# Complex product of the convolutions in three VectorE instructions, and five row buffers for the last experts

## The chip, the cores and the metric

One core of a Trainium2 chip runs the whole kernel. The metric is the device time of one execution in microseconds (us): the median of several runs. A program this long is decided by stages: TensorE (PE) multiplies matrices and reads its weights through a second track (PEld), VectorE (DVE), ScalarE (ACT) and GpSimd (POOL) do elementwise work, SyncE (SP) issues transfers, and GpSimd issues those with indices.

## The reference

Three layers on 1024 tokens of width 1024, all in float32. First an attention layer (MLA), then a layer of long convolutions (Hyena), then a block that mixes sliding window attention with a gated recurrence and ends in a mixture of 32 experts. The change touches two places.

The long convolution, done twice (`spec` comes from filters that a small network produces):

```python
def fft_long_conv(u, spec):
    L = u.shape[1]
    U = jnp.fft.rfft(u.astype(jnp.float32), n=2 * L, axis=1)
    return jnp.fft.irfft(U * spec, n=2 * L, axis=1)[:, :L].astype(u.dtype)
```

The experts: each token goes to two of 32 experts; an expert computes `silu(x @ w_gate) * (x @ w_up)` and multiplies it by `w_down`; the weighted rows are summed per token.

```python
def expert_block(args):
    xb, e = args
    h = jax.nn.silu(xb @ w_gate[e]) * (xb @ w_up[e])
    return h @ w_down[e]
```

## The kernel before

Nearly every matrix product is done as three: each float32 operand is split into a high part (rounded to the type that TensorE takes at full rate) and a low remainder. The helper `hilo` does this with a ScalarE copy (line 165) and a VectorE subtraction (line 166); `mm3` issues the three matmuls (lines 187 to 189).

The order of the instructions on each engine is fixed before the run, by a planner that simulates the program with costs of its own and issues what is ready there. `tc.issue_after(x)` adds an edge that keeps an engine's instructions behind `x` on that engine. Every engine works through its own list in order.

**Convolutions** (function `fwd`, `inv0`, `inv1`). Channels come in four chunks of 256 and two orders, eight units `n`. A forward transform `fwd(n, t)`, half of a unit (16 halves in all), makes four frequency tiles. For each, TensorE writes a PSUM tile `z` of 128 x 2 x 256 (real and imaginary parts) with 24 matmuls of 256 columns; there are four such PSUM tiles. SyncE loads the spectrum tile `K` (three buffers), and VectorE forms the complex product `yf` (lines 1177 to 1185): two half products into `B`, a full product, a subtraction for the real part, an addition for the imaginary part (with a sign for the last two tiles of eight). GpSimd then does six butterfly instructions on the four tiles (lines 1190 to 1196), `hilo` splits the results into `yh` and `yl`, and the inverse transform of the unit (`inv0` into `acc`, or `inv1` into `bcc`) takes them as matmul operands. The loop runs `fwd(n, 0)`, the inverse of unit n - 1, then `fwd(n, 1)`, so `fwd(n, 1)` and `fwd(n + 1, 0)` follow each other. When the convolutions end, TensorE goes on with the output projection (`oz`), whose weights `owr` are loaded and split at that time.

**Experts** (function `expert`, a generator that the loop at line 2069 steps so that experts overlap). For expert `e`, GpSimd gathers up to 112 rows of the normalised activations into `xg` (line 2003, two buffers), TensorE transposes them (line 2011), six weight blocks of 1 MB each are loaded and split, `ez` holds gate and up products, `dz` the two halves of the down product. ScalarE copies `dz`, scaled, from PSUM into the rows `y` (line 2047), and GpSimd adds the rows to the output with an indirect, accumulating transfer (line 2048). These additions go to the same tensor and are kept in order, each after the landing of the one before. PSUM has five banks for `ez` and `dz` together. From about the tenth expert on, `y` lies in one of three buffers of a weight pool (`praw[0]`, which holds no weights by then); before that it lies in a pair of its own (`px`).

In the last experts GpSimd's list holds only gathers and additions. After expert 31 a loop handles experts with more than 112 rows; its count is read at run time.

Of the kernel before, what the change touches and what calls it, by code (L numbers as in the profile page):

```python
# [8 lines left out]
F32 = mybir.dt.float32  # L9
# [3 lines left out]
AF = mybir.ActivationFunctionType  # L13
# [131 lines left out]
def _build(es, tc, nc, a, stop, dbg):  # L145
# [968 lines left out]
    with stc, ExitStack() as st:  # L1114
# [50 lines left out]
        def fwd(n, t):  # L1165

            c, o = units[n]
            y = []
            for ft in (t, 2 + t, 4 + t, 6 + t):
                z = ps.tile([P, 2, 256], F32, tag="z", name="z")  # L1170
                for q in range(2):
                    for kt in range(4):
                        mm3(z[:, q], *fwd_c(q, ft, kt), sd[n][q][0][:, kt], sd[n][q][1][:, kt], kt == 0, kt == 3)
                K = pk.tile([P, 2, 256], F32, tag="K", name="K", bufs=3)
                k_in.append(SY.dma_start(K, spec[c, o, ft].rearrange("p (r h) -> p r h", r=2)).ins)
                B = pk.tile([P, 2, 256], F32, tag="B", name="B")
                V.tensor_tensor(B[:, 0], z[:, 0], K[:, 1], ALU.mult)
                V.tensor_tensor(B[:, 1], z[:, 1], K[:, 0], ALU.mult)
                y.append(pyf.tile([P, 2, 256], F32, tag="yf", name="yf"))
                V.tensor_tensor(y[-1], z, K, ALU.mult)  # L1180
                V.tensor_tensor(y[-1][:, 0], y[-1][:, 0], y[-1][:, 1], ALU.subtract)
                if ft < 6:
                    V.tensor_tensor(y[-1][:, 1], B[:, 0], B[:, 1], ALU.add)
                else:
                    V.scalar_tensor_tensor(y[-1][:, 1], B[:, 0], -1.0, B[:, 1], ALU.mult, ALU.subtract)

            out = []
            E = V if n == 7 and t else G
            d = pyf.tile([P, 2, 256], F32, tag="yd", name="yd", bufs=1)
            E.tensor_tensor(d, y[1], y[3], ALU.add)  # L1190
            E.tensor_tensor(y[1], y[1], y[3], ALU.subtract)
            E.tensor_tensor(y[3], y[0], d, ALU.subtract)
            E.tensor_tensor(y[0], y[0], d, ALU.add)  # L1193
            d = pyf.tile([P, 2, 256], F32, tag="yd", name="yd", bufs=1)
            E.tensor_tensor(d, y[2], y[1], ALU.add)
            E.tensor_tensor(y[2], y[1], y[2], ALU.subtract)
            for x in (y[0], y[3], d, y[2]):
                yh = py.tile([P, 2, 256], F32R, tag="yh", name="yh")
                yl = py.tile([P, 2, 256], F32R, tag="yl", name="yl")
                hilo(yh, yl, x)  # L1200
                out.append((yh, yl))
            ys[n].append(out)
# [780 lines left out]
    def expert(px, pw, praw, ps, pst, xg, ix, wt, e, static=True):  # L1983

        def src(w):

            w = (w[e] if static else w[bass.ds(e, 1)].rearrange("o d f -> (o d) f")).rearrange("(p k) f -> p (k f)", p=P)
            return w[:, :2048], w[:, 2048:]

        def load(w):  # L1990
            n = n_raw[0]
            n_raw[0] += 1
            raw = slot_of(n).tile([P, 4, 512], F32, tag="ewr", name="ewr")
            if n in GATE:
                V.tensor_copy(raw[:, 0, :1], GATE[n])
            SY.dma_start(raw.rearrange("p k f -> p (k f)"), w)
            hi = pw[n % 5].tile([P, 4, 512], F32R, tag="ewh", name="ewh")
            lo = pw[n % 5].tile([P, 4, 512], F32R, tag="ewl", name="ewl")
            m = 1 if n < 5 else 2
            for k in range(0, 4, m):  # L2000
                hilo(hi[:, k:k + m], lo[:, k:k + m], raw[:, k:k + m])
            return hi, lo
        G.indirect_dma_start(out=xg[:BR], out_offset=None, in_=hn_d, in_offset=bass.IndirectOffsetOnAxis(ap=ix[:BR], axis=0),  # L2003
                             bounds_check=1023, oob_is_err=False)
        xh = px.tile([P, 8, P], F32R, tag="xh", name="xh")
        xl = px.tile([P, 8, P], F32R, tag="xl", name="xl")
        xk = xg.rearrange("t (p k) -> t k p", k=8)
        for k4 in range(2):
            z = pst.tile([P, 4, P], F32, tag="tr", name="tr")
            for k in range(4):  # L2010
                T.transpose(z[:, k], xk[:, k4 * 4 + k], ident)  # L2011
            hilo(xh[:, k4 * 4:k4 * 4 + 4], xl[:, k4 * 4:k4 * 4 + 4], z)
        yield
        zz = []
        for w in (wg, wu):
            z = ps.tile([P, 512], F32, tag="mm", name="ez")
            for k4 in range(2):
                wh, wl = load(src(w)[k4])
                for k in range(4):
                    kk = k4 * 4 + k  # L2020
                    mm3(z, xh[:, kk], xl[:, kk], wh[:, k], wl[:, k], kk == 0, kk == 7)
                if w is wg or k4 == 0:
                    yield
            zz.append(z)
        h = px.tile([P, 512], F32, tag="h", name="h", bufs=1)
        S.activation(h, zz[0], AF.Silu)
        V.tensor_tensor(h, h, zz[1], ALU.mult)  # L2027
        yield
        hh = px.tile([P, 4, P], F32R, tag="hh", name="hh", bufs=1)
        hl = px.tile([P, 4, P], F32R, tag="hl", name="hl", bufs=1)  # L2030
        z = pst.tile([P, 4, P], F32, tag="tr", name="tr")
        hk = h.rearrange("t (p k) -> t k p", k=4)
        for k in range(4):
            T.transpose(z[:, k], hk[:, k], ident)
        hilo(hh, hl, z)
        yield
        if n_raw[0] < 62:
            y = px.tile([P, 1024], F32, tag="y", name="y")
        else:
            y = praw[0].tile([P, 4, 512], F32, tag="ewr", name="y")[:, :2].rearrange("p a c -> p (a c)")  # L2040
        zz = [ps.tile([P, 512], F32, tag="mm", name="dz") for _ in range(2)]
        ws = [load(w) for w in src(wd)]
        for c, k in ((0, 0), (1, 0), (0, 1), (1, 1), (0, 2), (0, 3), (1, 2), (1, 3)):
            wh, wl = (x[:, k % 2 * 2 + c] for x in ws[k // 2])
            mm3(zz[c], hh[:, k], hl[:, k], wh, wl, k == 0, k == 3)
            if k == 3:
                S.activation(y[:BR, c * 512:(c + 1) * 512], zz[c][:BR], AF.Copy, scale=wt[:BR])
        G.indirect_dma_start(out=out_d, out_offset=bass.IndirectOffsetOnAxis(ap=ix[:BR], axis=0), in_=y[:BR], in_offset=None,  # L2048
                             bounds_check=1023, oob_is_err=False, compute_op=ALU.add)
        yield  # L2050

    ps = pool("ps8", 5, PSUM, st8)
    pst = pool("ps8t", 3, PSUM, st8)
    n_raw = [0]
    pw = [pool(f"ew{j}", 1, st=st8) for j in range(5)]

    def slot_of(n):
# [66 lines left out]
```

## Time and profile before

| | |
|---|---|
| median of 3 runs | 3218.64 us (3216.76 to 3223.12) |
| profiled execution | 3216.41 us, its span 3214.6 us |
| TensorE busy | 3053.7 us, 95% |
| VectorE busy | 2294.8 us, 71% |
| ScalarE busy | 1607.8 us, 50% |
| GpSimd busy | 892.2 us, 28% |
| mean granted TensorE clock | 0.985 |
| convolutions, from the first to the last `z` | about 1382 to 1664 us |
| experts, from the first gate product to the last addition | 2600.5 to 3202 us |

The shares are means over stages with different limits, so a stage is read by itself. Matmuls are pipelined: a row shows each from its start to its modelled end, and the next starts before that, so TensorE is not at its full rate wherever it is "busy". In the lists, a bracket says how long the engine was idle before an instruction and what ended that.

### The profile page before, as it was taken

The numbers are of one execution on the slowest core, as the hardware profiler recorded it, in microseconds if no ns is written. First come the engines' busy times: TensorE is split into PE (matmuls) and PEld (weight loads), VectorE is DVE, ScalarE is ACT, GpSimd is POOL, SyncE is SP. The second block draws the span as 40 slices with busy tenths as digits, with TensorE's granted clock in tenths as the row PEclk, the third lists the DMA queues.
The fourth block names the chain that finished last, engine by engine and source line by source line (L and its number), as shares of the span: only waits on it lengthen the run. The fifth ranks groups of instructions, "written<-read, shape, count | busy, mean of one in ns | idle before, by whom it ended". The sixth has DMA issues, their size and how long they took to land. (4 is left out here: it accounts for less than half of the span.)

```text
span 3214.6 us, 49325 instructions
## 1 busy us (share of the span) xinstructions
PE 3053.7 (95%) x18106; PEld 2681.9 (83%) x18106; DVE 2294.8 (71%) x4600; ACT 1607.8 (50%) x2762; POOL 892.2 (28%) x825
## 2 busy tenths in 40 slices
PE   7998999999999899999988999999999989999997
PEld 3898879998887788899987999888878978878775
DVE  4575236666667988889896667577646689889885
ACT  3333347666653444411134446455423368778785
POOL 3771042775001444456650000000000025331111
PEclk9999999999999999999999999999999989999998
DMA  8752222331224222174335311321444689999995
GB/s 276 214 193 86 79 92 63 91 99 61 83 92 120 85 101 99 60 255 143 106 108 189 98 52 53 107 66 60 124 148 163 214 302 365 340 345 365 372 363 168
DMA packets 287019, 514.58 MB, mean 160 GB/s; under 512 B 49594, under 2 KB 201826, under 8 KB 262200
## 3 DMA queue, kind: packets, MB, share of 16 engines
q1 hardware_dynamic: 273608, 478.60, 43.8%
q0 software_dynamic: 13168, 32.81, 3.8%
q8 instruction: 143, 2.34, 0.3%
q14 instruction: 100, 0.82, 0.1%
HBM read 431.28 MB, written 92.61 MB: 163 GB/s over the span
## 5 line engine op out<-in xcount | busy, mean ns | idle before, releaser
L166 DVE TENSOR_TENSOR ewl<-ewr,ewh 128x1024 fp32r<-128x1024 f32 (+1 forms) x394 | 447.1, 1192 | 49.2 <-ACT ewh L165 48.3
L165 ACT ACTIVATE ewh<-ewr 128x1024 fp32r<-128x1024 f32 (+1 forms) x394 | 377.8, 1034 | 33.2 <-PE dz L189 24.6
L187 PE MATMUL ez<-ewh,xh 128*128 128x512 f32 x512 | 203.8, 401 | 10.4 <-DVE h L2027 5.2
L188 PE MATMUL ez<-ewl,xh 128*128 128x512 f32 x512 | 203.9, 398 | 3.5 <-DVE ewl L166 3.3
L189 PE MATMUL ez<-ewh,xl 128*128 128x512 f32 x512 | 201.3, 393 | 0.0
L187 PE MATMUL cz<-cTh,w5h 128*128 128x512 f32 x384 | 152.5, 399 | 0.8 <-ACT w5h L165 0.8
L188 PE MATMUL cz<-cTl,w5h 128*128 128x512 f32 x384 | 152.5, 397 | 0.0
L189 PE MATMUL cz<-cTh,w5l 128*128 128x512 f32 x384 | 150.2, 395 | 0.0
L166 DVE TENSOR_TENSOR ptl<-tr,pth 128x512 fp32r<-128x512 f32 x160 | 108.0, 686 | 49.0 <-ACT pth L165 48.4
L2003 POOL DMA_INDIRECT xg<-hn_d,idx x32 | 51.0, 1594 | 313.2 <-PE tr L2011 311.8
L798 DVE TENSOR_SCALAR_CACHE_REDUCE pr<-s 128x512 f32<-128x512 f32 (+1 forms) x192 | 109.6, 597 | 34.5 <-PE s L797 18.6
L187 PEld LDWEIGHTS ez<-ewh,xh 128*128 128x128 f32 x512 | 97.2, 190 | 34.1 <-ACT xh L165 7.6
L768 POOL TENSOR_SCALAR adaw<-adaw,cond 128x256 f32<-128x256 f32 x112 | 103.9, 940 | 54.4 <-DMA adaw<-in_ada_w_dram 54.4
L188 PEld LDWEIGHTS ez<-ewl,xh 128*128 128x128 f32 x512 | 97.4, 190 | 23.8 <-DVE ewl L166 4.9
L165 ACT ACTIVATE pth<-tr 128x512 fp32r<-128x512 f32 x160 | 91.6, 592 | 49.5 <-PE tr L815 47.9
L189 PEld LDWEIGHTS ez<-ewh,xl 128*128 128x128 f32 x512 | 97.0, 190 | 19.9
L187 PE MATMUL oz<-owh,oh 128*128 128x512 f32 x256 | 102.1, 403 | 10.7 <-ACT oh L165 5.1
L165 ACT ACTIVATE yh<-yf 128x512 fp32r<-128x512 f32 x48 | 28.5, 625 | 157.3 <-POOL yf L1193 141.7
L802 ACT ACTIVATE pr<-pr,mx 128x1280 f32<-128x1280 f32 x64 | 87.2, 1362 | 32.7 <-DVE mx L801 32.4
L189 PE MATMUL oz<-owh,ol 128*128 128x512 f32 x256 | 101.0, 399 | 1.5 <-DVE ol L166 1.5
L188 PE MATMUL oz<-owl,oh 128*128 128x512 f32 x256 | 101.9, 400 | 0.5 <-DVE owl L166 0.5
L188 PE MATMUL dz<-ewl,hh 128*128 128x512 f32 x256 | 100.5, 393 | 0.0
(770 smaller groups left out, 10896.0 us busy)
## 6 DMA issues: line engine op xcount, KB each, us to landing
ewr<-in_w_up_experts_dram SPq DMA_DIRECT2D x64, 1024.0 KB
ewr<-in_w_gate_experts_dram SPq DMA_DIRECT2D x64, 1024.0 KB
ewr<-in_w_down_experts_dram SPq DMA_DIRECT2D x64, 1024.0 KB
spec<-so SPq DMA_DIRECT2D x64, 256.0 KB
adaw<-in_ada_w_dram SPq DMA_DIRECT2D x64, 256.0 KB
hwr<-in_hy_w_in_dram SPq DMA_DIRECT2D x64, 256.0 KB
K<-spec SPq DMA_DIRECT2D x64, 256.0 KB
w5r<-in_w_in_dram SPq DMA_DIRECT2D x60, 256.0 KB
```

What stands on the lines that cost most here:

```text
L165: S.activation(hi, x, AF.Copy)
L166: V.tensor_tensor(lo, x, rd(hi), ALU.subtract)
L187: T.matmul(ps, lh, rh, start=first, stop=False)
L188: T.matmul(ps, lh, rl, start=False, stop=False)
L189: return T.matmul(ps, ll, rh, start=False, stop=last)
L768: G.tensor_scalar(w[:, i], w[:, i], cond[:, k + i, 0:1], None, ALU.mult)
L798: V.tensor_scalar(pr[:, k0:k0 + n], z[:, :n], 1.0, None, ALU.mult, ALU.max, accum_out=mx[:, c:c + 1])
L802: S.activation(pr, pr, AF.Exp, scale=SC, bias=mx[:, 3:4], accum_out=sm)
L2003: G.indirect_dma_start(out=xg[:BR], out_offset=None, in_=hn_d, in_offset=bass.IndirectOffsetOnAxis(ap=ix[:BR], axis=0), bounds_check=1023, ...
```

## The change

Convolutions: the spectrum tile gets a third column block of 256, which takes a negated copy of the imaginary part (for the last two tiles of eight, the negated real part, and the imaginary part is negated in place). ScalarE makes these copies. VectorE then forms the product in three instructions over 512 elements each: real part of `z` times the pair, imaginary part times the turned pair (written back into `z`, in PSUM), and the sum. The buffer `B` is gone.

Experts: the additions are collected in a list `done`. From the gather that is issued when 28 additions are listed on (experts 30 and 31), a gather is kept behind the sixth addition from the end of the list, which is that of expert 22 or 23. Of the experts from 24 on, 26, 28 and 31 take their rows `y` from the pair `px`, the others from the three buffers of `praw[0]`.

```diff
-                K = pk.tile([P, 2, 256], F32, tag="K", name="K", bufs=3)
-                k_in.append(SY.dma_start(K, spec[c, o, ft].rearrange("p (r h) -> p r h", r=2)).ins)
-                B = pk.tile([P, 2, 256], F32, tag="B", name="B")
-                V.tensor_tensor(B[:, 0], z[:, 0], K[:, 1], ALU.mult)
-                V.tensor_tensor(B[:, 1], z[:, 1], K[:, 0], ALU.mult)
+                K = pk.tile([P, 3, 256], F32, tag="K", name="K", bufs=3)
+                u = 1 if ft < 6 else 0
+                k_in.append(SY.dma_start(K[:, u:u + 2], spec[c, o, ft].rearrange("p (r h) -> p r h", r=2)).ins)
+                if u:
+                    S.activation(K[:, 0], K[:, 2], AF.Copy, scale=-1.0)
+                else:
+                    S.activation(K[:, 2], K[:, 0], AF.Copy, scale=-1.0)
+                    S.activation(K[:, 1], K[:, 1], AF.Copy, scale=-1.0)
                 y.append(pyf.tile([P, 2, 256], F32, tag="yf", name="yf"))
-                V.tensor_tensor(y[-1], z, K, ALU.mult)
-                V.tensor_tensor(y[-1][:, 0], y[-1][:, 0], y[-1][:, 1], ALU.subtract)
-                if ft < 6:
-                    V.tensor_tensor(y[-1][:, 1], B[:, 0], B[:, 1], ALU.add)
-                else:
-                    V.scalar_tensor_tensor(y[-1][:, 1], B[:, 0], -1.0, B[:, 1], ALU.mult, ALU.subtract)
+                V.tensor_tensor(y[-1], z[:, 0:1].broadcast_to([P, 2, 256]), K[:, u:u + 2], ALU.mult)
+                V.tensor_tensor(z, z[:, 1:2].broadcast_to([P, 2, 256]), K[:, 1 - u:3 - u], ALU.mult)
+                V.tensor_tensor(y[-1], z, y[-1], ALU.add)
...
-        G.indirect_dma_start(out=xg[:BR], out_offset=None, in_=hn_d, in_offset=bass.IndirectOffsetOnAxis(ap=ix[:BR], axis=0),
-                             bounds_check=1023, oob_is_err=False)
+        with tc.issue_after(done[-6].ins) if static and len(done) > 27 else ExitStack():
+            G.indirect_dma_start(out=xg[:BR], out_offset=None, in_=hn_d, in_offset=bass.IndirectOffsetOnAxis(ap=ix[:BR], axis=0),
+                                 bounds_check=1023, oob_is_err=False)
...
-        if n_raw[0] < 62:
+        if n_raw[0] < 62 or (static and e > 23 and e % 5 in (1, 3)):
             y = px.tile([P, 1024], F32, tag="y", name="y")
...
-        G.indirect_dma_start(out=out_d, ...
+        done.append(G.indirect_dma_start(out=out_d, ...
```

## Rows read from the trace of the kernel before

**Rows 1.** Stretch: busy us (instructions) of PE, PEld, DVE, ACT, POOL; clock, DMA.
```profile
1400.00:1672.00 272.00, 255.40 (x2072) 251.92 (x2070) 244.69 (x412) 50.75 (x83) 167.97 (x132) 0.99 0.38 123
```

**Rows 2.** TensorE's waits, 1400 to 1672: us in total, times, longest.
```profile
PE bcc L189 <- DVE yl L166: 6.2, 5, 1.9
PE z L187 <- DVE yf L1180: 4.3, 3, 1.7
PE acc L188 <- DVE yl L166: 3.3, 4, 1.8
PE bcc L187 <- ACT yh L165: 1.9, 1, 1.9
```

**Rows 3.** VectorE's groups, 1380 to 1690: busy us, mean ns; last, line 1180's durations.
```profile
L1180 DVE TENSOR_TENSOR yf<-z,K 128x512 f32<-128x512 f32 x64 | 43.5, 679 | 0.0
L1183 DVE TENSOR_TENSOR yf<-B 128x256 f32<-128x256 f32 x48 | 42.1, 876 | 1.1
...
L1181 DVE TENSOR_TENSOR yf<-yf 128x256 f32<-128x256 f32 x64 | 39.0, 609 | 1.2
L1177 DVE TENSOR_TENSOR B<-z,K 128x256 f32<-128x256 f32 x64 | 26.9, 421 | 7.8 <-PE z L189 3.5 <-DMA K<-spec 0.9
L1178 DVE TENSOR_TENSOR B<-z,K 128x256 f32<-128x256 f32 x64 | 26.4, 413 | 0.0
...
L1185 DVE SCALAR_TENSOR_TENSOR yf<-B 128x256 f32<-128x256 f32 x16 | 6.8, 423 | 0.5
...
L1180 DVE TENSOR_TENSOR yf<-z,K x64: 673/680/683, 1385.7 to 1669.2; 128x512 f32<-128x512 f32 x64
```

**Rows 4.** ScalarE: its waits; a 256-element copy (min/median/max); one butterfly chain in order.
```profile
ACT yh L165 <- POOL yf L1193: 141.7, 14, 20.0
...
L165 ACT ACTIVATE owh<-owr x18: 402/418/632, 1674.7 to 1699.5; 128x256 fp32r<-128x256 f32 x16, 128x512 fp32r<-128x512 f32 x2
...
1528.21 1.29 POOL L1190 TENSOR_TENSOR yd<-yf 128x512 f32<-128x512 f32 x1 [2.78 <-DVE yf L1185]
...
1536.77 0.63 ACT L165 ACTIVATE yh<-yf 128x512 fp32r<-128x512 f32 x1 [0.78 <-POOL yf L1196]
```

**Rows 5.** Instructions in order of time, end of the convolutions: start, us, engine, line.
```profile
1663.58 0.28 PE L188 MATMUL z<-sd1l,fc 128*128 128x256 f32 x1
1663.70 0.28 PE L189 MATMUL z<-sd1h,fc 128*128 128x256 f32 x1
...
1668.55 0.42 DVE L1177 TENSOR_TENSOR B<-z,K 128x256 f32<-128x256 f32 x1
...
1699.62 0.79 PE L187 MATMUL oz<-owh,oh 128*128 128x512 f32 x1 [5.09 <-ACT owh L165]
```

**Rows 6.** Stretch of the experts, columns as in rows 1.
```profile
2650.00:3150.00 500.00, 486.89 (x2266) 401.21 (x2266) 437.67 (x433) 395.11 (x483) 132.78 (x90) 1.00 0.98 359
```

**Rows 7.** GpSimd's last instructions in order of time; last, the transposes of `xg`.
```profile
3099.74 1.93 POOL L2003 DMA_INDIRECT xg<-hn_d,idx  x1 [18.62 <-PE tr L2011]
3101.97 2.44 POOL L2048 DMA_INDIRECT out_dram<-y,idx  x1 [0.30 <-issue]
...
3195.02 1.45 POOL L2048 DMA_INDIRECT out_dram<-y,idx  x1 [5.16 <-DMA out_dram<-y,idx]
3201.51 1.45 POOL L2048 DMA_INDIRECT out_dram<-y,idx  x1 [5.04 <-DMA out_dram<-y,idx]
...
L2011 PE MATMUL tr<-ident,xg x256: 270/274/453, 2598.1 to 3138.1; 128*128 128x128 f32 x128
```

**Rows 8.** ScalarE's row copies and two matmuls of the last experts, in order of time.
```profile
3144.70 0.50 PE L187 MATMUL dz<-ewh,hh 128*128 128x512 f32 x1 [0.78 <-DVE h L2027]
...
3177.22 0.50 PE L187 MATMUL ez<-ewh,xh 128*128 128x512 f32 x1 [1.92 <-ACT h L2026]
...
3178.96 1.26 ACT L2047 ACTIVATE y<-dz,wgt 112x512 f32<-112x512 f32 x2
...
3197.15 0.69 ACT L2047 ACTIVATE y<-dz,wgt 112x512 f32<-112x512 f32 x1 [0.62 <-PE dz L189]
```

More of the change, by code (lines that the diff above doesn't have):

```diff
@@ L2047, in expert @@
                 S.activation(y[:BR, c * 512:(c + 1) * 512], zz[c][:BR], AF.Copy, scale=wt[:BR])
-        G.indirect_dma_start(out=out_d, out_offset=bass.IndirectOffsetOnAxis(ap=ix[:BR], axis=0), in_=y[:BR], in_offset=None,
-                             bounds_check=1023, oob_is_err=False, compute_op=ALU.add)
+        done.append(G.indirect_dma_start(out=out_d, out_offset=bass.IndirectOffsetOnAxis(ap=ix[:BR], axis=0), in_=y[:BR],
+                                         in_offset=None, bounds_check=1023, oob_is_err=False, compute_op=ALU.add))
         yield
@@ L2053, in _build @@
     pst = pool("ps8t", 3, PSUM, st8)
-    n_raw = [0]
+    n_raw, done = [0], []
     pw = [pool(f"ew{j}", 1, st=st8) for j in range(5)]
```

## The prediction

> **What bounds the kernel now.** I read the busy times of the engines in stretches first, then who waited for whom on TensorE, then the instruction groups of VectorE, and last the single instructions in order of time at the two places that the change touches.
>
> In the convolutions TensorE and VectorE are both nearly full: from 1400 to 1672 us TensorE is busy 255.4 of 272 us and VectorE 244.7, while ScalarE has 50.8 [rows 1]. TensorE's true shortfall is larger than the 16.6 us that this leaves, because a matmul's modelled end overlaps the next: in a full stretch one starts every 0.12 us though each is shown as 0.28 [rows 5]. The 2072 matmuls of the stretch [rows 1] at 0.12 are 248.6 us, so 23.4 us of the 272 are lost. Four waits explain most of it: for the low halves `yl` (6.2 and 3.3 us), for the read of `z` by line 1180 (4.3) and for `yh` (1.9), together 15.7 us in 13 pieces [rows 2]. Each piece hides 0.28 - 0.12 = 0.16 us more, 2.1 us in all, and the granted clock of 0.99 over the stretch [rows 1] is about 2.7 us. All but the `yh` wait (1.9) are for VectorE: it is late, and TensorE waits.
>
> In the experts, from 2650 to 3150 us, the DMA engines are busy 0.98 of the time [rows 6], so the weight stream paces the middle, and only what lies behind the last weights can shorten the end. There the additions into the output follow one another: the last two start 6.49 us apart, the last one 5.04 us after the engine went idle, released by the landing of the one before [rows 7].
>
> **The complex product.** Removed per transform tile: two half products, one full product, a subtraction and an addition (or negated subtraction). Over 64 tiles these are 26.9 + 26.4 + 43.5 + 39.0 + 42.1 + 6.8 = 184.7 us [rows 3]. Added: three instructions of 512 elements, each with one operand in PSUM and one in SBUF. The nearest row is line 1180, the same shape and kinds of operand, 0.68 us with 0.683 the longest of 64 [rows 3]. 3 x 64 x 0.679 = 130.4 us, so VectorE has 54 us less to do, 50 of them in the 59/64 or so of the tiles that lie in the stretch; its load there falls from 244.7 to about 195 us.
>
> One of the three writes into PSUM, which no row shows for VectorE. From below: lines 1178 and 1180 differ by 266 ns for 256 elements, so 512 elements stream in no less than 0.53 us, which adds 9 us of relief. From above: the mean of line 1183 exceeds that of line 1185, which does the same number of elements, by 0.876 - 0.423 = 0.45 us [rows 3]; if each PSUM write were as much longer, 29 us of the 54 would go and 25 remain. I take 0.68, the row of the same shape.
>
> The large share of the 54 us is contention that goes: lines 1181 and 1183 have both operands in SBUF and take 609 and 876 ns on average where line 1185 takes 423 [rows 3]. The tile is held longer in PSUM, 3 x 0.68 = 2.04 us against 0.42 + 0.41 + 0.68 = 1.51, but TensorE fills one in 24 x 0.12 = 2.9 us and there are four, so this costs nothing while VectorE keeps up.
>
> [...]
>
> ScalarE gets 48 copies of 256 elements for the first six frequency tiles of each set of eight and 2 x 16 for the others: 80 x 0.418 = 33 us, by the same size in [rows 4]. It has 221 idle us in the stretch [rows 1], 141.7 of them waiting at `yh` for line 1193 on GpSimd [rows 4], so its time is hidden. What is queued behind a copy on ScalarE is `yh`, the data of the next unit and the output copies; a copy waits only for its spectrum load, issued three tiles (3 x 2.9 = 8.6 us) ahead. If the cover were gone, each product would wait for a copy behind a `yh`; the price is the third rival. SyncE issues the same 64 loads.
>
> What this gives on TensorE: 15.7 + 2.1 + 2.7 = 20.5 us can go at most. I keep a third of it as still lost, because the chain behind the last product of a half runs through GpSimd: from its first butterfly at 1528.21 to the end of the last `yh` at 1537.40 [rows 4] are 9.2 us, then 0.7 for `yl`, against the 96 x 0.12 = 11.5 us that TensorE spends on the next half. It fits, with 1.6 us to spare, once VectorE has no backlog. So **-13.7 us** (ends: 4.3 + 0.5 for the `z` waits alone, and 23.4). At the end of the stage the last tile is complete at 1663.98 and its product starts at 1668.55, a backlog of 4.6 us [rows 5] that should go; but TensorE then waits 5.09 us up to 1699.62 for converted output weights [rows 5], whose loads need not move. I count 0 here, with 4.6 as the other end.
>
> **The last experts.** Experts 26, 28 and 31 move to the free pair of row buffers; 24, 25, 27, 29 and 30 keep the three large ones, so a row's buffer no longer waits for the addition of three experts before. Before, addition 22 starts at 3101.97 behind the gather of expert 31 [rows 7], and the rows of expert 28, whose down product begins at 3144.70, are copied out only at 3178.96 [rows 8]. After, gather 30 stands behind addition 22 and gather 31 behind 23, in GpSimd's queue, where by then only gathers and additions stand. That wait costs nothing up to 38 us: gather 31 starts at 3099.74 and its rows are transposed from about 3138 on [rows 7], while two more additions in front of it are 2 x 6.5 = 13 us. Past that cover it would push expert 31 back one for one.
>
> What is gained: addition 30 can start when its rows are ready and not behind a late chain, and the last addition when its own are: 3197.15 + 0.69 + 0.3 for the hand-over is 3198.2 against 3201.51 [rows 7, 8], **-3.3 us**. The matmul at 3177.22 waited 1.92 us for a PSUM bank [rows 8], while the finished product of expert 28 still held two of the five; I take **-1 us** of it (ends 0 and 2.1), since the last weights are still being split then. The part as a whole: 0 to -5.4.
>
> Sum: -13.7 - 0 - 3.3 - 1 = -18 us. The profiled execution took 3216.4 us (span 3214.6 and 1.8 around it), so 3198.4; the median of the runs is 2.2 us above it, so the forecast is **3200.6 us**.
>
> **Rivals.**
> *GpSimd's chain is the limit.* The `yl` and `yh` waits stay, because the 9.2 us of butterflies [rows 4] and not VectorE's backlog set them; only the `z` waits with their hidden part, 4.8 us, and 0 to 4.3 of the tail go: 3209.5 to 3213.8. For it: ScalarE waits 141.7 us for that chain [rows 4]. Against it: the chain fits in 11.5 us, and most of TensorE's waits name `yl`, not `yh` [rows 2].
> *Given back at the weights.* The convolutions end earlier, the output weights do not, and the wait of 5.09 us [rows 5] grows by the gain; the tail is paced by the weights' conversion: 3216 to 3218.6. Against it: later stages wait for TensorE and not for loads until the experts.
> *Slower: the negated half stands behind `yh`.* ScalarE runs in order. If the fixed order puts a copy behind a `yh` that waits for GpSimd, VectorE stops at the second product for up to the 9.2 us chain. With 195 us of work in about 258, VectorE can lose 63/14 = 4.5 us in each of the 14 halves that wait [rows 4] before TensorE feels it; beyond that 4.7 us a half are exposed. If half of them are, 7 x 4.7 = 33 us against the gain of 18: 3234. It decides from 4.5 us per half. Against it: the copy is ready 8.6 us ahead, before the chain ends.
> *The added order does not hold.* If the rows' buffers are not what delays the additions, the last part gives 0: 3204.9, still inside the forecast's own range.
>
> **Chances.** The forecast 0.63 (own range 3190 to 3209, the last case in it), GpSimd's chain 0.18, given back 0.08, the slower case 0.08, and 0.03 for a new order of other instructions, since the planner places all of them by its own costs. A measurement of this kernel can tell 0.2%, 6.4 us. Faster by more: 0.63 + 0.13 + 0.02 = 0.78; within: 0.05 + 0.08 = 0.13; slower: 0.08 + 0.01 = 0.09. The range runs from 3185 (3218.6 - 23.4 - 4.6 - 5.4) to 3216, where most of what is left above is the slower case.
>
> **What would show it.** Right: three VectorE groups of about 0.68 us per tile and none above 0.75; VectorE at 195 us or so in the stage; TensorE's waits for `yl` and `z` below 6 us; the last `z` followed by its product within 1 us; the last addition within 1 us of its rows; additions 22 and 23 before gathers 30 and 31. Wrong: a PSUM write well above 0.75 us, VectorE waiting for ScalarE at the second product, TensorE waits now named after GpSimd or `yh`, or a longer wait for the output weights near the stage's end.

## The result and the profile after

The changed kernel takes **3188.5 us** (median of 4 runs, 3184.7 to 3191.5), the kernel before in the same comparison 3217.7 us (3214.0 to 3223.1, 4 runs): a ratio of 0.9907, 95% interval 0.9891 to 0.9923. The forecast was 3200.6 us: the direction was right, the time lies inside the range (3185 to 3216), and the gain is 29 us where 18 were forecast, just outside the forecast's own range (3190 to 3209). The profiled executions are 3216.41 and 3189.40 us.

Where the 27 us went is read from six instructions in each trace; the differences add up from stage to stage.

| start or end of | before, us | after, us | stage before | stage after | difference |
|---|---|---|---|---|---|
| first `z` starts | 1381.9 | 1380.8 | | | -1.1 |
| last `z` starts | 1663.7 | 1650.2 | 281.8 | 269.4 | -12.4 |
| last `oz` ends | 1796.8 | 1775.1 | 133.1 | 124.9 | -8.2 |
| first `ez` starts | 2600.5 | 2581.5 | 803.7 | 806.4 | +2.7 |
| last `dz` ends | 3197.1 | 3170.7 | 596.6 | 589.2 | -7.4 |
| last addition starts | 3201.5 | 3174.6 | 4.4 | 3.9 | -0.5 |

The first row says nothing about the change: over the twelve profiles of this document the first `z` starts between 1374.0 and 1383.7 us, though all of them run the same code up to there.

**The convolutions.** The stretch of [rows 1], now 258 us long, with the same columns:

```profile
1400.00:1658.00 258.00, 251.00 (x2067) 249.72 (x2066) 211.30 (x299) 77.78 (x159) 166.76 (x132) 0.99 0.41 133
```

At 0.12 us each, 2067 matmuls are 248.0 us, so 10.0 us of the stretch are lost where it was 23.4. TensorE's waits (us in total, times, longest) answer to [rows 2]; all of 0.7 us or more are here:

```profile
PE z L187 <- DVE yf L1186: 4.7, 3, 3.0
PE bcc L187 <- ACT yh L165: 2.2, 1, 2.2
```

The 9.5 us for `yl` are gone. VectorE's groups answer to [rows 3]; the three product instructions are 131.2 us in all, where the five were 184.7:

```profile
L166 DVE TENSOR_TENSOR yl<-yf,yh 128x512 fp32r<-128x512 f32 x48 | 47.7, 1011 | 10.4 <-ACT yh L165 10.3
L1185 DVE TENSOR_TENSOR z<-z,K 128x512 f32<-128x512 f32 x64 | 44.0, 691 | 1.9
L1186 DVE TENSOR_TENSOR yf<-z,yf 128x512 f32<-128x512 f32 x64 | 43.7, 684 | 1.1
L1184 DVE TENSOR_TENSOR yf<-z,K 128x512 f32<-128x512 f32 x64 | 43.5, 682 | 19.9 <-DMA K<-spec 11.2 <-PE z L189 6.3 <-ACT K L1182 2.1
```

Line 1185 is the one that writes into PSUM: 691 ns on average. The bracket of line 1184 shows what VectorE now waits for: the spectrum loads (11.2 us, 7.5 of them once), and ScalarE's copies for only 2.1 us in 64 tiles. ScalarE's waits, beside [rows 4]:

```profile
ACT K L1179 <- DMA K<-spec: 72.9, 27, 10.8
ACT yh L165 <- POOL yf L1194: 29.0, 11, 7.4
```

ScalarE still waits, but for its spectrum tile more than for GpSimd (141.7 us in [rows 4]).

**The end of the convolutions**, beside [rows 5]: VectorE's and TensorE's instructions in order of time (start, us; the bracket is the idle time before and its releaser), and SyncE's loads of the output weights.

```profile
1649.77 0.68 DVE L1184 TENSOR_TENSOR yf<-z,K 128x512 f32<-128x512 f32 x1
1652.07 0.68 DVE L1185 TENSOR_TENSOR z<-z,K 128x512 f32<-128x512 f32 x1
1653.27 0.68 DVE L1184 TENSOR_TENSOR yf<-z,K 128x512 f32<-128x512 f32 x1
...
1649.21 0.38 SPq L848 DMA_DIRECT2D owr<-in_hy_w_out_dram  x1
1651.86 3.37 SPq L848 DMA_DIRECT2D owr<-in_hy_w_out_dram  x4
...
1683.41 1.22 PE L187 MATMUL oz<-owh,oh 128*128 128x512 f32 x2 [4.72 <-ACT owh L165]
```

The last tile is complete at 1650.5 and its product starts at 1653.27: a backlog of 2.8 us where it was 4.6. The weight loads came forward with the stage (the first one started at 1668.31 before). TensorE's waits from the last `z` to the last `oz`, first of the kernel before:

```profile
PE oz L187 <- ACT oh L165: 5.1, 2, 4.4
PE oz L187 <- ACT owh L165: 5.1, 1, 5.1
PE bcc L187 <- DVE ym L1256: 2.0, 1, 2.0
PE oz L189 <- DVE ol L166: 1.5, 1, 1.5
PE bcc L189 <- DVE yl L166: 0.6, 1, 0.6
PE oz L188 <- DVE owl L166: 0.5, 1, 0.5
```

and of the changed kernel:

```profile
PE oz L187 <- ACT owh L165: 4.7, 1, 4.7
PE oz L189 <- DVE ol L166: 2.2, 2, 2.0
PE oz L187 <- ACT oh L165: 1.6, 2, 0.8
PE bcc L187 <- DVE ym L1257: 0.6, 1, 0.6
```

The wait for the weights (`owh`) is nearly the same; those for the data (`oh`, `ym`, `ol`, `yl`) fell from 9.2 to 4.4 us. The stretches behind the last `z`, of the kernel before (columns as in [rows 1]):

```profile
1664.00:1684.00 20.00, 14.70 (x85) 11.95 (x85) 19.71 (x35) 11.07 (x23) 9.60 (x9) 0.83 0.78 237
1684.00:1704.00 20.00, 14.91 (x89) 13.20 (x88) 14.12 (x29) 6.75 (x16) 0.00 (x0) 0.83 0.82 275
1704.00:1796.40 92.40, 87.98 (x404) 72.73 (x403) 64.11 (x144) 41.85 (x91) 0.00 (x0) 0.98 0.45 141
```

and of the changed kernel:

```profile
1650.50:1670.00 19.50, 16.12 (x100) 14.54 (x99) 19.40 (x35) 11.74 (x25) 4.63 (x5) 0.82 0.74 230
1670.00:1690.00 20.00, 15.28 (x89) 13.32 (x88) 11.74 (x24) 5.44 (x12) 0.00 (x0) 0.91 0.89 291
1690.00:1774.70 84.70, 83.70 (x392) 69.09 (x391) 63.03 (x143) 41.16 (x90) 0.00 (x0) 1.00 0.45 145
```

The clock column is a mean over each stretch; the records of both traces hold two levels, 1.00 and 0.50. Behind the last `z` the clock stands at 0.50 from 1676.9 to 1683.7, from 1697.4 to 1704.2 and from 1724.7 to 1728.1 us before, and from 1662.5 to 1669.3 and from 1683.0 to 1686.4 us after: 17.1 us and 10.2. In the three stretches before, TensorE's gaps are 5.3, 5.1 and 4.4 us and the clock 0.83, 0.83 and 0.98; after, the gaps are 3.4, 4.7 and 1.0 us and the clock 0.82, 0.91 and 1.00. Over the three stretches TensorE is idle for 14.8 us before and 9.1 after, and busy for 117.6 and 115.1 us with 578 and 581 matmuls: 5.7 us of the 8.2 are waits, and 2.5 are the same matmuls done in less time.

**The last experts.** GpSimd's last instructions, beside [rows 7]:

```profile
3063.37 2.12 POOL L2050 DMA_INDIRECT out_dram<-y,idx  x1 [8.63 <-ACT y L2049]
3065.79 1.16 POOL L2005 DMA_INDIRECT xg<-hn_d,idx  x1 [0.30 <-issue]
3075.39 1.49 POOL L2050 DMA_INDIRECT out_dram<-y,idx  x1 [8.44 <-ACT ewh L165]
3080.32 1.94 POOL L2005 DMA_INDIRECT xg<-hn_d,idx  x1 [3.45 <-PE tr L2013]
...
3168.22 1.45 POOL L2050 DMA_INDIRECT out_dram<-y,idx  x1 [13.50 <-ACT y L2049]
3174.62 1.45 POOL L2050 DMA_INDIRECT out_dram<-y,idx  x1 [4.95 <-issue]
```

The order is the announced one: additions 22 and 23 stand before gathers 30 and 31. The wait of 1.92 us in [rows 8] is gone with others: from the first `ez` to the last `dz` TensorE's waits sum to 11.8 us (17.1 before). Up to the first matmul of expert 27 both kernels take the same time from the first `ez`, 491.8 us before and 491.4 after; from there to the last `dz` it is 104.8 and 97.8 us, so the whole gain lies in the last five experts.

What changed there is when ScalarE copies a finished product out of PSUM. Expert 28 in the kernel before, whose product starts at 3144.70 and is copied at 3178.96 [rows 8]: an addition, the last matmul of the product, and what ScalarE does just ahead of the copy.

```profile
3148.14 1.45 POOL L2048 DMA_INDIRECT out_dram<-y,idx  x1 [10.70 <-ACT y L2047]
3150.57 0.39 PE L189 MATMUL dz<-ewh,hl 128*128 128x512 f32 x1
3177.07 2.00 ACT L165 ACTIVATE ewh<-ewr 128x1024 fp32r<-128x1024 f32 x2
```

The last matmul and the copies of the same expert in the changed kernel:

```profile
3124.57 0.39 PE L189 MATMUL dz<-ewh,hl 128*128 128x512 f32 x1
3128.54 1.26 ACT L2049 ACTIVATE y<-dz,wgt 112x512 f32<-112x512 f32 x2
```

Before, the product is complete at 3150.96. The row buffer, which expert 25 had, is free even earlier: the addition that starts at 3148.14 is that of expert 26, and it stands behind the landing of expert 25's. Yet the copies start 28 us later, directly behind conversions of weights in ScalarE's list. So on the chip this copy does not wait for its buffer; its place in the list is late. The same holds for experts 25 to 31: the addition that frees the buffer has landed 8 to 33 us before the first copy. With five buffers the copies stand earlier: the second copy of experts 25 to 29 starts 36, 36, 32, 29 and 14 us after the end of the product before, and 23, 12, 19, 4 and 9 us after it in the changed kernel. Until then the product holds two of the five PSUM banks. That the planner places the copy by when its own simulation has the buffer free is argued from what it does with three and with five buffers; its simulated times are not on record.

### The profile page after: what moved, and what is told of

Read it like the earlier page. It is cut to its first block, busy times and chain, and to the rows that moved or that the text cites. A ratio compares the mean times of both kernels' runs of the same rounds, so it can differ in the third digit from the quotient of the medians.

```text
span 3187.4 us, 49365 instructions
## 1 busy us (share of the span) xinstructions
PE 3050.4 (96%) x18106; PEld 2684.2 (84%) x18106; DVE 2258.5 (71%) x4472; ACT 1634.3 (51%) x2842; POOL 884.9 (28%) x825
## 5 line engine op out<-in xcount | busy, mean ns | idle before, releaser
L2050 POOL DMA_INDIRECT out_dram<-y,idx x32 | 62.3, 1946 | 134.1 <-ACT y L2049 84.8
```

Source lines behind the costliest of these rows:

```text
L2050: done.append(G.indirect_dma_start(out=out_d, out_offset=bass.IndirectOffsetOnAxis(ap=ix[:BR], axis=0), in_=y[:BR], in_offset=None, bounds ...
```

## The experiments

Ratios are against the kernel before in the same comparison (its medians there are 3215.7 to 3219.6 us); in parentheses the 95% interval. "z" is the time from the first to the last `z`, "to ez" from there to the first `ez`, "experts" from there to the end of the last `dz`, each from one profiled execution.

| kernel | median, us | ratio | z | to ez | experts |
|---|---|---|---|---|---|
| before | 3217.7 | | 281.8 | 936.8 | 596.6 |
| changed | 3188.5 | 0.9907 (0.9891, 0.9923) | 269.4 | 931.3 | 589.2 |
| product alone | 3197.4 | 0.9941 (0.9929, 0.9954) | 269.9 | 933.1 | 598.8 |
| experts alone | 3210.8 | 0.9977 (0.9968, 0.9986) | 282.6 | 939.2 | 591.8 |
| one product more | 3189.7 | 0.9921 (0.9908, 0.9934) | 275.7 | 935.2 | 584.0 |
| two butterflies more | 3191.6 | 0.9923 (0.9910, 0.9936) | 273.6 | 937.1 | 584.7 |
| product in SBUF | 3199.9 | 0.9938 (0.9925, 0.9952) | 276.7 | 932.1 | 589.8 |
| stores on GpSimd | 3189.0 | 0.9909 (0.9893, 0.9924) | 267.7 | 930.4 | 588.2 |
| buffers without edge | 3190.9 | 0.9911 (0.9896, 0.9926) | 270.2 | 933.0 | 589.8 |
| edge without buffers | 3205.9 | 0.9951 (0.9936, 0.9965) | 269.1 | 935.0 | 597.8 |
| two more edges | 3189.2 | 0.9911 (0.9896, 0.9926) | 268.9 | 934.1 | 590.1 |
| an edge on every gather | 3206.0 | 0.9962 (0.9949, 0.9976) | 267.2 | 934.2 | 608.5 |

The stages of kernels with the same code there show how far one profile can be trusted: "z" is 267.2 to 270.2 in six kernels with the new product, and "to ez" 931.3 to 935.0 in the same six. Differences below about 4 us in one stage say little.

**The two parts, each alone.** The convolutions' part of the diff without the experts' part, and the reverse.

> The complex product in three VectorE instructions, the last experts as before. If the gain of the convolutions (12.4 us up to the last transform tile and some 6.5 us behind it) comes from VectorE's relief and the two parts are independent: about 3198 to 3200 us against 3218 for before, ratio 0.994, and the experts from the first gate product to the last down product take 596 us as before (2600.5 to 3196.7). If the gain behind the last tile or in the experts comes from the other part: above 3205.

> Five row buffers and the ordered gathers alone, the convolutions as before. If the parts are independent: 8 us less than before, about 3210, ratio 0.9975, with the experts 589 us long from the first gate product to the last down product. If the experts gained only because the convolutions ended earlier: same as before, 3218.

The product alone gives 0.59%, the experts 0.23%, together 0.82% where both in one kernel give 0.93% (the intervals overlap): the parts add up. In the trace the product keeps "z" (-11.9 us) and most of "to ez" (-3.7), and gives nothing in the experts; the other part gains only there (-4.8).

**More work on VectorE, more work on GpSimd.** The first product instruction done twice (44 us more for VectorE):

```diff
                 V.tensor_tensor(y[-1], z[:, 0:1].broadcast_to([P, 2, 256]), K[:, u:u + 2], ALU.mult)
+                V.tensor_tensor(y[-1], z[:, 0:1].broadcast_to([P, 2, 256]), K[:, u:u + 2], ALU.mult)
```

> The changed kernel with the first of the three product instructions done twice into the same place: 64 x 0.68 = 44 us more for VectorE, 0.6 us more on the chain behind each half. VectorE's backlog as the cause: its load in the convolutions goes back from 211 to about 250 us of the stretch, the waits of TensorE for the low halves and for z return, 8 to 14 us slower than the changed kernel (3197 to 3202). GpSimd's chain as the limit: not more than 14 x 0.6 = 8 us, with waits named after ScalarE's yh. No limit at VectorE at all: unchanged, 3188.

The first butterfly done three times (2.6 us more in the chain behind each half's last product):

```diff
             E.tensor_tensor(d, y[1], y[3], ALU.add)
+            E.tensor_tensor(d, y[1], y[3], ALU.add)
+            E.tensor_tensor(d, y[1], y[3], ALU.add)
```

> The changed kernel with the first butterfly of each half done three times on GpSimd: 2 x 1.3 = 2.6 us more in the chain from the last product to yh, in each of 15 halves. GpSimd's chain as the limit: 14 x 2.6 = 36 us slower than the changed kernel (3224). VectorE's backlog as the cause, with the chain fitting into the next half with 1.6 us to spare: up to 14 x 1.0 = 14 us slower, more likely 2 to 8 (3190 to 3197), with the new waits of TensorE at yh and yl.

Both lengthen the stage, by 6.3 and 4.2 us, and the way from there to the experts, by 3.9 and 5.8, of which the first is at the edge of what equal kernels differ. The stretches of the two, which end at the last `z` (columns as in [rows 1]): VectorE is nearly as full as before in the first (0.89 of the stretch, 0.90 before), and GpSimd 32 us fuller in the second.

```profile
1400.00:1654.00 254.00, 244.74 (x1994) 242.63 (x1994) 226.71 (x343) 73.37 (x152) 155.99 (x129) 0.99 0.38 124
```

```profile
1400.00:1653.00 253.00, 245.71 (x2002) 243.21 (x2001) 210.91 (x286) 72.99 (x150) 198.99 (x156) 0.99 0.38 125
```

Neither theory, VectorE's backlog or GpSimd's chain, holds alone. 44 us of VectorE, most of what the change took away, bring back about half of the 12.4 us; 39 us of GpSimd (15 halves of 2.6) bring back a third. Nor is either addition pure: the doubled product lengthens the chain behind each half by 0.7 us, and the butterflies stretch VectorE's `yl` (56.1 us for 48 of them, 47.7 in the changed kernel), so the share of each engine is not separated. The totals hide the loss: both kernels are 5 us shorter in the experts, whose order the planner laid out differently. By the totals alone both experiments would say "no effect".

**The second product in SBUF.** It is written over `K`, so the third instruction has both operands in SBUF.

```diff
-                V.tensor_tensor(z, z[:, 1:2].broadcast_to([P, 2, 256]), K[:, 1 - u:3 - u], ALU.mult)
-                V.tensor_tensor(y[-1], z, y[-1], ALU.add)
+                V.tensor_tensor(K[:, 1 - u:3 - u], z[:, 1:2].broadcast_to([P, 2, 256]), K[:, 1 - u:3 - u], ALU.mult)
+                V.tensor_tensor(y[-1], K[:, 1 - u:3 - u], y[-1], ALU.add)
```

> The changed kernel, but the second product is written over the spectrum tile in SBUF and not over z in PSUM: the third instruction then has both operands in SBUF. If such instructions are stretched by GpSimd (1183 took 876 ns where 423 was the undisturbed time): the third takes 0.9 to 1.2 us on average and not 0.68, VectorE gets 15 to 30 us more, and the kernel loses 2 to 8 us against the changed one (3190 to 3196). If only the number of instructions counts: 0.68 us each and unchanged, 3188.

The third instruction's row, and its durations (min/median/max):

```profile
L1186 DVE TENSOR_TENSOR yf<-K,yf 128x512 f32<-128x512 f32 x64 | 58.2, 911 | 1.1
...
L1186 DVE TENSOR_TENSOR yf<-K,yf x64: 674/692/1780, 1384.4 to 1663.1; 128x512 f32<-128x512 f32 x64
```

The same addition takes 684 ns with one operand in PSUM and 911 with both in SBUF; the median is nearly the same, but single ones reach 1780. Writing `z` into PSUM, the step whose price was unknown, is what keeps the third instruction out of this: 14.5 us of VectorE. The stage is 7.3 us longer. That this is all VectorE's lost time is not shown: 44 us of added work cost only 6.3 above, and here GpSimd is slowed too (from the first to the last `z` it is busy for 176.8 us, 170.5 in the changed kernel). The longer hold on `K` is not the reason, since VectorE's wait for spectrum loads is no longer (10.5 and 11.2 us). The total, 3199.9 us, is above the expected 3190 to 3196.

In the trace of the kernel before, instructions with both operands in SBUF are longer beside GpSimd, and those with one operand in PSUM are not. Between 1380 and 1690 us line 1183 takes 420 ns on average (427 at most) in the 21 cases in which no GpSimd instruction runs beside it, and 1231 in the 27 in which one does; line 1181 takes 421 in 36 cases and 851 in 28; line 1180, with one operand in PSUM, takes 679 either way. With the product in SBUF the shortest third instruction takes 674 ns (673 in the changed kernel), and the longest 1780 (693): 1.1 us longer, which is less than the 1.29 us of one butterfly [rows 4].

**Stores on GpSimd.** The one long wait for a spectrum tile (7.5 us) stands behind stores in SyncE's list that wait for GpSimd (10.2 us in three waits between 1500 and 1530 us); here the stores of all units but the last go to GpSimd's own queue.

```diff
-                    SY.dma_start(z2_d[c // 3][2 * c + m - c // 3 * 6, :, h * 512:(h + 1) * 512], gt[h])
+                    (SY if n == 7 else G).dma_start(z2_d[c // 3][2 * c + m - c // 3 * 6, :, h * 512:(h + 1) * 512], gt[h])
```

> The changed kernel with the stores of the convolutions' results (all but the last unit) issued by GpSimd itself and not by SyncE, so that the loads of the spectrum no longer stand behind a store that waits for GpSimd (a load came 7.5 us late to VectorE once, and TensorE then waited 2.2 us). If these late loads are what is left of the loss: 2 to 5 us faster than the changed kernel, 3184 to 3187. If GpSimd's own list is the tighter one: 12 issues of about 0.55 us in its chain, 0 to 7 us slower.

The edit does what it should, since VectorE's wait for spectrum loads falls from 11.2 to 3.5 us:

```profile
L1184 DVE TENSOR_TENSOR yf<-z,K 128x512 f32<-128x512 f32 x64 | 43.6, 682 | 17.0 <-PE z L189 9.9 <-ACT K L1182 3.6 <-DMA K<-spec 3.5
```

TensorE's wait for `z` stays at 4.7 us, and the time shows no difference that can be told: 3189.0 against 3188.5 us. The late loads cost nothing that shows.

**The experts' part taken apart.** The five buffers without the edge, and the edge with the three old buffers:

```diff
-        with tc.issue_after(done[-6].ins) if static and len(done) > 27 else ExitStack():
+        with ExitStack():
```

> The changed kernel without the edge that keeps the gathers of experts 30 and 31 behind additions 22 and 23; five row buffers stay. If the buffers make the gain of the experts (TensorE no longer waits for PSUM banks that undelivered rows hold): 3188 to 3190. If the order of GpSimd's list is what makes it: 5 to 8 us slower than the changed kernel, 3194 to 3196.

```diff
-        if n_raw[0] < 62 or (static and e > 23 and e % 5 in (1, 3)):
+        if n_raw[0] < 62:
```

> The changed kernel with the edge but with three row buffers for all of the last experts. If the buffers make the gain: 5 to 8 us slower than the changed kernel, 3194 to 3196, and TensorE's waits in the last 110 us come back (9 us). If the order makes it: 3188 to 3190.

TensorE's gain is the buffers': experts in 589.8 us without the edge, 597.8 with the edge alone. TensorE's waits in that stage are 11.5 and 17.8 us (11.8 in the changed kernel, 18.4 with the product alone). ScalarE's copies of expert 28, first without the edge and then with the edge alone, where they are merged with those of expert 29:

```profile
3129.44 1.28 ACT L2049 ACTIVATE y<-dz,wgt 112x512 f32<-112x512 f32 x2
...
3170.62 2.40 ACT L2049 ACTIVATE y<-dz,wgt 112x512 f32<-112x512 f32 x4
```

The product is complete at 3125.85 and 3136.93: the copies come 4 and 34 us later. The edge alone took 3205.9 us in total where 3194 to 3196 was expected; of the 17 us between its profile and that of the changed kernel, 8.6 are the experts, 3.4 the end, and 5 lie ahead of the experts, where the code is the same.

The edge acts on the very end. The last addition starts 4.4 us after the last `dz` before and 3.5 with the product alone, 6.3 with the buffers alone (gathers 30 and 31 still stand ahead, and the last additions follow one another 6.6 to 7.1 us apart), 7.3 with the edge alone, 3.9 with both. So the edge is worth about 2.4 us on top of the buffers, which two medians 2.5 us apart with overlapping intervals bear out but don't prove; it takes back what the buffers alone lose there, and the two together gain nothing over the product alone at this place.

**More edges.** In the two kernels with added work, additions 6 and 7 stood ahead of gathers 12 and 13, and a stall of TensorE in expert 12 was missing. The first kernel gives the changed one this order by edges; the second keeps every gather from expert 12 on behind the fourth addition from the end, with five buffers from there.

```diff
-        with tc.issue_after(done[-6].ins) if static and len(done) > 27 else ExitStack():
+        with tc.issue_after(done[-4 if e < 14 else -6].ins) if static and (e in (12, 13) or e > 29) else ExitStack():
```

> The changed kernel with the same kind of edge at two earlier places: the gathers of experts 12 and 13 are kept behind the additions of experts 6 and 7 on GpSimd, and those of 30 and 31 stay behind the sixth addition from the end. Theory (a gather ahead of an addition holds row buffers, and TensorE loses what that delays): TensorE's stall in expert 12 (waits of 1.8 us for ewh and 0.9 us for ewl) goes, first gate product of expert 13 at 227 us after that of expert 0 instead of 232; the 4 to 5 us stay until the end: experts 584 us instead of 589, total 3184 us on the scale of this comparison's 3188.5 for the changed kernel. Rival (the two changed kernels with this order won their 5 us by the convolutions' end, not by the order): 232 us at expert 13 and no difference at the end. Second rival: given back at expert 27 to 33, total within 1 us of the changed kernel.

```diff
-        with tc.issue_after(done[-6].ins) if static and len(done) > 27 else ExitStack():
+        with tc.issue_after(done[-4].ins) if static and e > 11 else ExitStack():
...
-        if n_raw[0] < 62 or (static and e > 23 and e % 5 in (1, 3)):
+        if n_raw[0] < 62 or (static and e > 11 and e % 5 in (1, 3)):
```

> The changed kernel with an edge on every gather from expert 12 on: each stands behind the fourth addition from the end of the list, so that GpSimd's list alternates one gather and one addition to the end; five row buffers from expert 12 on instead of 24. Theory (row buffers set when ScalarE can empty PSUM): no stall in expert 13, none at the end, so 227 us at expert 13, 98 us from expert 27 to the end, total 3183 to 3185 us. Rival (gathers that wait for additions come late): an addition lands 5 to 6 us after the one before, and a gather behind it gives its rows later than the transposes want them; then TensorE waits for xg or its transposes in several experts, and the total is over 3190 us.

With two more edges the stall goes: expert 13 begins 228.0 us after expert 0 instead of 232.2. But expert 17 begins at 304.1 against 303.9: given back within four experts, in a stretch whose DMA engines are busy 0.98 of the time [rows 6]. So the order of these two gathers is not what makes the other two kernels 5 us shorter; their weight loads are laid out differently too (the 79th is issued 320.9 and 321.7 us after the first, 326.0 in the changed kernel), and what of that decides stays open. No version here beats the changed kernel.

With an edge on every gather the experts take 19 us longer, and not for the rival's reason: TensorE's only waits for gathered rows, 5.7 us in both kernels, lie ahead of the first `ez`. Between 2850 and 3060 us ScalarE has a wait of which the changed kernel shows none there:

```profile
ACT y L2049 <- PE dz L189: 16.5, 8, 4.2
```

The row copies stand in ScalarE's list where they wait for `dz`, what is queued behind them waits too, and the last of the 192 weight loads is issued 17 us later after the first than in the changed kernel. That the new place of the copies is the cause is argued, not shown; which edge set it off was not tried.

## Why the prediction was right, and where it was not

- **The product's size: right.** 131.2 us, forecast 130.4; the write into PSUM 691 ns, forecast 680. Neither bound (0.53 us, or 0.45 more) was needed. The measured relief is 53.5 us. Of it, 33.7 us are what lines 1181 and 1183 took above the 423 ns of line 1185, and 19.8 us remain without that.
- **VectorE's load: wrong by 16 us.** 211 us, not 195. 8.6 us of this are the low halves `yl`: their two groups went from 41.6 and 11.3 us to 47.7 and 13.8, the first from 877 to 1011 ns each. The step took contention as something that goes with the instructions removed, and let the instructions with two SBUF operands that stay, `yl` among them, cost what they did. More of `yl` now runs beside GpSimd: 39 of the 64 instructions, at 1162 ns on average, where it was 18 at 1225; the others take 678 ns, and 681 before. Why more of them do is open. It is not simply contention handed on: with the product in SBUF, where the third instruction is stretched again, the first group is still at 1001 ns, and with one product more at 907. Some of the rest is where the two stretches cut the work off; it was not separated.
- **The convolutions: right in size, half right in reason.** -12.4 us in the profile (-13.1 between the means of six kernels with the new product, 269.1, and two without, 282.2), forecast -13.7. The backlog reading ("VectorE is late, and TensorE waits") and the rival *GpSimd's chain* were put as alternatives; the two experiments with added work show that TensorE feels both, but not in which shares.
- **The copies on ScalarE: right.** 27 us more busy time, hidden; VectorE waited for them 2.1 us. The slower rival (3234) needed waits of over 4.5 us per half and met none.
- **The end of the convolutions, counted as 0: missed.** -8.2 us to the last `oz`, -5.5 to the first `ez`. The step said that TensorE waits "for converted output weights, whose loads need not move". They moved with the stage: the first by 19 us (1668.31, now 1649.21), the others by some 16. The wait for `owh` stayed at 5 us, and those for data behind VectorE's backlog shrank, so that all waits there went from 14.8 to 9.1 us; the other 2.5 us are matmuls done in less time, with 10.2 us at a granted clock of 0.50 where it was 17.1. The gain is well outside the noise: from the last `z` to the last `oz` the six kernels with the new product take 124.9 to 125.6 us, the two without 133.1 and 132.5. To the first `ez` it is -4.6 us between the means of the same kernels. The bound named there (4.6) was too small as well. The rival *given back at the weights* is refuted with it. The 2.7 us that are lost again between `oz` and `ez` lie within what equal kernels differ there.
- **The last experts: the places were right, the sizes and half of the mechanism wrong.** Waiting for a PSUM bank was taken as -1 us (0 to -2.1), because one wait of 1.92 us stood in the rows. It was a family: with five row buffers, 5.3 us of TensorE's waits go, and the experts are 7.4 us shorter (4.8 and 9.6 in the two other pairs with and without this part). The step said that a row's buffer waits for the addition of three experts before. The trace of before shows no copy of experts 25 to 31 that waits for its buffer; the copies are late in ScalarE's list, and five buffers move them forward. The sign stood in the rows, a copy at 3178.96 for a product that is complete at 3150.96, and was read as a wait. ScalarE's longest wait at these copies, 5.2 us from 3190.6, ends when the first half of expert 31's own product is complete (3195.8); the addition that frees its buffer had landed at 3187.7. The last addition was put at -3.3 us; its distance to the last `dz` fell by 0.5, and the product alone has 3.5 without this part. It is still 3.1 us behind its rows (3171.55 to 3174.62), because the rows of experts 30 and 31 are finished 3.6 us apart and the additions start 6.4 apart.
- **"The added order does not hold"**: half true. The order does nothing for TensorE; the buffers do. That rival's price (3204.9) assumed that the whole part would then be lost.
- **The sum.** Convolutions -12.4 (forecast -13.7), their end -5.5 net (0), experts to the last `dz` -7.4 (-1), last addition -0.5 (-3.3), start -1.1: -27 against -18. Two misses of 5 and 6 us, both at places priced by one visible wait. Both lie outside the bounds given for them (8.2 us to the last `oz` where 4.6 was the end, 7.9 for the experts and their end where it was 5.4); that the time still falls into the range is owed to the convolutions, which stayed 11 us short of their own end of 23.4, and in so far it is luck.
- **The signs.** The three product groups at 0.68 to 0.69 us, waits for `yl` and `z` of 4.7 us, and the order of additions and gathers came as announced. VectorE at 195 us, the last product within 1 us of its `z` (2.8) and the last addition within 1 us of its rows (3.1) did not.

## What to carry to other kernels

A wait at the end of one stage says what is late there now, not what it will be worth when everything ahead comes earlier: look at which of the loads behind it are themselves waiting for the stage. Where a finished result is copied out late, compare three times: when the result is complete, when the buffer it goes to is free, and when the copy starts. If the copy is later than both, its place in the engine's list holds it, and a further buffer can still help because the planner then orders the list differently; TensorE's share of the delay, 5.3 us here, was spread over small waits, none above 1.9 us. And when an added-work experiment leaves the total unchanged, compare stage by stage before calling it no effect: a planner may pay for it elsewhere.

## What was not expected of the hardware

- VectorE writes 512 elements into PSUM in 691 ns where SBUF takes 682, when one operand is in PSUM in either case.
- A VectorE instruction with two SBUF operands is stretched by different amounts as the work around it changes: `yl` went from 877 to 1011 ns when the product instructions with both operands in SBUF were gone, to 1183 with the two extra butterflies on GpSimd and to 907 with one product more on VectorE; with the third product instruction in SBUF it stayed at 1001.
